# A decoder layer's head: x loaded first and turned at once, ada loads of 256 columns, five of eight rows summed on VectorE

## Chip, core, metric

One core of one Trainium2 chip runs the whole kernel. The metric is the device time of one execution in microseconds (us), the median of the runs shown. The engines are TensorE (PE; its weight loads PEld), VectorE (DVE), ScalarE (ACT), GpSimd (POOL) and SyncE (SP), which issues nearly all loads.

## What is computed

One decoder layer on x of 256 tokens by 1024 features in float32. The change is in the first lines: six vectors of 1024 come from the conditioning vector c, two of them (shift and scale) modulate the normed x, and the result u goes into one combined projection.

```
c_act = jax.nn.silu(c)
mod = (c_act @ w_ada[l] + b_ada[l])[:, None, :]
sh1, sc1, g1, sh2, sc2, g2 = jnp.split(mod, 6, axis=-1)
u = modulate(rmsnorm(h, norm1[l]), sh1, sc1)      # x * (1.0 + scale) + shift
h = h + g1 * token_mixer(u, w_in[l], ...)         # proj = u @ w_in, then retention, latent attention, merge
u = modulate(rmsnorm(h, norm2[l]), sh2, sc2)
h = h + g2 * hier_moe(u, ...)                     # top group, top-2 experts, SwiGLU
return rmsnorm(h, final_norm)
```

## The kernel before

The kernel is one long program for five in-order queues. The features are cut into eight chunks k of 128. The **head** is the loop `for k in range(8)` with what stands ahead of it: for each k it needs u of chunk k (256 tokens), made from x's chunk turned by TensorE (`x_turned`), from shift and scale of that chunk (`ada_mm`, `mod_of`), and from `u_of`, in which ScalarE scales (L444) and rounds to a high part (L446) and VectorE subtracts to a low part (L447). The weights of w_in are split in the same way (`split`: ScalarE L458 the high part, VectorE L459 the low part). Each product is three matmuls, high by high, low by high, high by low. In round k there are twelve matmuls of 352 columns (`mm3`, L373 to L375, in two halves n = 0 and 1) and twelve of 256 columns (`feat_mm`, L525 to L527).

Shift and scale of a chunk are a product of c_act with a 1024 x 256 piece of w_ada: one 1 MB buffer that holds 128 columns of shift and 128 of scale for all eight rows j (128 numbers of c each). TensorE does it as eight matmuls (L419) in four column groups that run side by side, the column of c_act being one of 32 columns, the rest zero; VectorE copies the result (L422), TensorE turns it (L435), VectorE reduces it over the four groups (L437) and applies norm and bias (L438, L440).

Loads stand in a list in program order and are issued by SP as buffers come free (27 buffers of 1 MB). At the start: ada of chunk 0, then x, then for each k ada of chunk k + 1 and the two pieces of w_in (`e0`, `e1`). On TensorE nine matmuls on ones, and eight more behind the first ada matmuls (`keep_warm`, `WARM0`), do no useful work. The order on TensorE in the loop is written out by hand, that on VectorE and ScalarE ahead of the loop too; in the loop a scheduler orders VectorE and ScalarE. The rest of the layer (attention, retention, merge, experts) isn't edited.

Of the kernel before, what the change touches and what calls it, by code (L numbers as in the profile page):

```python
# [43 lines left out]

WARM0 = 9, 8
WARM2 = 2
WARM3 = 1
WARM4 = 0
# [12 lines left out]
def const_tables():  # L61
# [143 lines left out]
def body(ctx, tc, A, out, plan=None):  # L205
# [207 lines left out]

    def ada_mm(k, pa):

        ev = ev_s.t[:, 256 * (k % 2):256 * (k % 2 + 1)]
        t = LD.get(("ada", k)).t.rearrange("p (k n) -> p k n", k=8)
        for j in range(8):
            i = T.matmul(pa.t[32 * (j % 4):32 * (j % 4) + 32, :256], csb[:, j, :], t[:, j, :], start=j < 4, stop=j >= 4,  # L419
                         skip_group_check=True, tile_position=(0, 32 * (j % 4)))  # L420
        LD.done(("ada", k))
        V.tensor_copy(ev, pa.t[:, :256])  # L422
        return ev, i.ins

    def x_turned(k):
        px = bank()
        for b in range(2):
            T.transpose(px.t[:, b * 128:(b + 1) * 128], xh[:, b, k * 128:(k + 1) * 128], ident)
        return px

    last_u = [None]

    def mod_of(k, pa, ev):
# [3 lines left out]
        V.tensor_reduce(sc, pa.t[:, 256:512].rearrange("p (i j r) -> p i j r", i=2, j=4)[:, :, :, 0], AX.X, ALU.add)  # L437
        V.scalar_tensor_tensor(acl[:, k:k + 1], sc[:, 1:2], bsc1[:, k:k + 1], colt[:, 8 + k:9 + k], op0=ALU.add,  # L438
                               op1=ALU.mult)
        V.tensor_add(shc[:, k:k + 1], sc[:, 0:1], colt[:, 16 + k:17 + k])  # L440
        pa.free()

    def u_of(k, px):
        last_u[0] = S.activation(uf[:, k, :], px.t[:, 0:256], AF.Identity, bias=shc[:, k:k + 1], scale=acl[:, k:k + 1]).ins  # L444
# [3 lines left out]
        px.free()  # L448

# [57 lines left out]

    scaled(0, 0, 128)
    scaled(1, 0, 128)
    scaled(0, 128, 384)  # L510
    scaled(1, 128, 1024)
    u_of(0, x_turned(0))
# [18 lines left out]
    for k in range(8):  # L531
# [6 lines left out]

        if 0 < k < 7:
            px, pa = x_turned(k + 1), bank()  # L540
            ev = ada_mm(k + 1, pa)[0]
        for n in range(2):
            s, hi, lo = hl[n]
            for b in range(2):
                mm3(eacc[n][b].t[:, :352], u_blk(k, b), (hi[:, 0, :], lo[:, 0, :]), k == 0, k == 7)
            s.free()
            if (n, k) == (0, 0):
                start.close()
                early = ExitStack()
                early.enter_context(tc.manual_schedule(engines={T.engine}))  # L550
                px = x_turned(1)
# [1128 lines left out]
```

## Time and profile before

| | |
|---|---|
| median of 3 runs | 524.14 us (523.97 to 524.57) |
| profiled execution | 524.77 us, its span 523.0 us, mean granted clock 0.993 |
| TensorE busy | 496.2 us, 95% of the span |
| VectorE, ScalarE busy | 282.5 us (54%), 197.9 us (38%) |
| moved by DMA | 175.42 MB, 335 GB/s in the mean |

The profile is of one execution; times in it run from the start of its span. A busy TensorE isn't one at its peak, since matmuls are pipelined and overlap in the rows. [...]

### The profile page before, as it was taken

How to read it: one execution, taken by the hardware profiler on the slowest of the kernel's cores; microseconds unless marked ns; L12 is line 12 of the kernel's file. 1: busy time of each engine (PE TensorE's matmuls, PEld its weight loads, DVE VectorE, ACT ScalarE, POOL GpSimd, SP SyncE). 2: the span in 40 equal slices, each digit the busy share in tenths (PEclk: the TensorE clock that was granted, in tenths of full speed). 3: DMA queues.
4: the chain of work that ended last, by engine and by line, in shares of the span. 5: the costliest groups of instructions: out<-in, count | busy, mean ns of one | idle time of the engine just before them, and what ended most of it. 6: DMA issues, size and time to landing. Idle time of an engine off the chain costs nothing.

```text
span 523.0 us, 9335 instructions
## 1 busy us (share of the span) xinstructions
PE 496.2 (95%) x3819; PEld 357.8 (68%) x3819; DVE 282.5 (54%) x524; ACT 197.9 (38%) x365; POOL 57.2 (11%) x50
## 2 busy tenths in 40 slices
PE   6999999999999999999999999999999989898984
PEld 2778999997887899999999887443334343434332
DVE  2455789883796978968956846413031213122113
ACT  2545873445677544556434524202020211111013
POOL 1000311411000001119800000000000000000000
PEclk8999999999999999999999999999999999999998
DMA  9999899788867781998697998999999999998994
GB/s 272 322 319 362 290 362 398 280 330 313 312 236 248 264 312 74 370 356 310 236 387 268 358 346 308 416 397 422 419 419 419 419 418 419 419 420 328 388 350 130
DMA packets 69778, 175.42 MB, mean 335 GB/s; under 512 B 5437, under 2 KB 27106, under 8 KB 60006
## 3 DMA queue, kind: packets, MB, share of 16 engines
q1 hardware_dynamic: 67136, 174.01, 89.7%
q10 hardware_dynamic: 2598, 0.79, 0.6%
q8 instruction: 31, 0.51, 0.4%
q14 instruction: 13, 0.11, 0.1%
HBM read 173.74 MB, written 1.05 MB: 334 GB/s over the span
## 4 chain that ended last, share of the span: by engine, by line
PE 80%; DVE 7%; DMA 4%; ACT 2%; SPq 2%; issue 2%; POOL 1%; ACTq 0%; DVEq 0%; POOLq 0%
PE b L1379 11%; PE b L527 6%; PE b L525 6%; PE b L526 6%; PE b L1482 6%; PE b L373 5%; PE b L375 5%; PE b L1320 5%; PE b L374 5%; PE b L1491 5%; DVE s L459 2%; DMA s<-in_w 2%; DMA s<-in_w_in 2%; PE b L1331 1%; PE b L1513 1%
## 5 line engine op out<-in xcount | busy, mean ns | idle before, releaser
L459 DVE TENSOR_TENSOR s<-s,s 128x1024 fp32r<-128x1024 f32 (+2 forms) x92 | 107.9, 1185 | 44.6 <-ACT s L458 44.4
L458 ACT ACTIVATE s<-s 128x1024 fp32r<-128x1024 f32 (+2 forms) x92 | 83.4, 921 | 85.1 <-PE b L527 50.4
L525 PE MATMUL b<-s,s 128*128 128x256 f32 x384 | 110.1, 287 | 0.0
L527 PE MATMUL b<-s,s 128*128 128x256 f32 x384 | 109.1, 284 | 0.7 <-DVE s L459 0.7
L526 PE MATMUL b<-s,s 128*128 128x256 f32 x384 | 108.7, 283 | 0.0
L527 PEld LDWEIGHTS b<-s,s 128*128 128x128 f32 x384 | 73.5, 192 | 1.4 <-DVE s L459 1.4
L526 PEld LDWEIGHTS b<-s,s 128*128 128x128 f32 x384 | 73.7, 192 | 0.4 <-issue 0.2
L525 PEld LDWEIGHTS b<-s,s 128*128 128x128 f32 x384 | 73.6, 192 | 0.4 <-issue 0.2
L1379 PE MATMUL b<-s,s 128*32 128x256 f32 x1024 | 61.8, 381 | 1.0 <-DMA s<-in_w 1.0
L1379 PEld LDWEIGHTS b<-s,s 128*32 128x32 f32 x1024 | 32.2, 110 | 32.9 <-issue 10.4
L373 PE MATMUL b<-s,s 128*128 128x512 f32 (+2 forms) x130 | 50.9, 392 | 1.1 <-ACT s L458 1.0
L375 PE MATMUL b<-s,s 128*128 128x512 f32 (+2 forms) x130 | 48.8, 375 | 0.0
L374 PE MATMUL b<-s,s 128*128 128x512 f32 (+2 forms) x130 | 48.3, 372 | 0.0
L1043 DVE SCALAR_TENSOR_TENSOR s<-s,cs,s 128x1024 f32<-128x1024 f32 x32 | 41.4, 1293 | 0.3
L1463 ACT ACTIVATE wr<-b 128x256 f32<-128x256 f32 x8 | 3.1, 383 | 87.0 <-PE b L1379 82.2
L1482 PE MATMUL b<-s,wr 128*32 128x512 f32 x224 | 32.8, 596 | 0.0
L1320 PE MATMUL b<-s,sml 128*128 128x512 f32 x56 | 27.2, 605 | 5.3 <-DVE sml L1316 5.3
L373 PEld LDWEIGHTS b<-s,s 128*128 128x128 f32 x130 | 24.5, 188 | 10.7 <-ACT s L458 4.4
L1314 DVE TENSOR_TENSOR S<-cst,rk 128x128 f32<-128x128 f32 x16 | 4.1, 287 | 48.9 <-PE b L1433 48.9
L1464 DVE SCALAR_TENSOR_TENSOR wr<-wr,b 128x256 f32<-128x256 f32 x8 | 3.3, 416 | 45.4 <-ACT wr L1463 45.4
L1111 POOL TENSOR_TENSOR s<-s,s 128x1024 f32<-128x1024 f32 x8 | 26.2, 3308 | 13.5 <-DMA s<-in_w_out 13.5
L375 PEld LDWEIGHTS b<-s,s 128*128 128x128 f32 x130 | 24.4, 188 | 4.5 <-DVE s L459 0.5
(254 smaller groups left out, 663.0 us busy)
## 6 DMA issues: line engine op xcount, KB each, us to landing
s<-in_w SPq DMA_DIRECT2D x92, 1024.0 KB
s<-in_w_in SPq DMA_DIRECT2D x22, 1024.0 KB
s<-in_w_ada SPq DMA_DIRECT2D x16, 1024.0 KB
s<-in_w_ada SPq DMA_DIRECT2D x16, 512.0 KB
s<-in_w_mla_o SPq DMA_DIRECT2D x4, 1024.0 KB
s<-in_w_ret_o SPq DMA_DIRECT2D x4, 1024.0 KB
s<-in_w_out SPq DMA_DIRECT2D x4, 1024.0 KB
s<-in_w SPq DMA_DIRECT2D x6, 512.0 KB
```

Source lines behind the costliest of these rows:

```text
L373: T.matmul(o, l[0], r[0], start=start, stop=False, skip_group_check=True)
L374: T.matmul(o, l[1], r[0], start=False, stop=False, skip_group_check=True)
L375: return T.matmul(o, l[0], r[1], start=False, stop=stop, skip_group_check=True)
L458: S.activation(hi, src, AF.Copy)
L459: V.tensor_tensor(lo, src, hi, ALU.subtract)
L525: T.matmul(o, hi[:, f], mh, start=k == 0 and c == 0, stop=False, skip_group_check=True)
L526: T.matmul(o, hi[:, f], ml, start=False, stop=False, skip_group_check=True)
L527: T.matmul(o, lo[:, f], mh, start=False, stop=k == 7, skip_group_check=True)
L1043: V.scalar_tensor_tensor(a, t[:, kk, :], cs[:, k:k + 1], a, op0=ALU.mult, op1=ALU.add)
L1320: T.matmul(pg[k4].t, Sr[:, b], hp[:, b, 4 * k4:4 * k4 + 4, :].rearrange("p k q -> p (k q)"), start=b == 0, stop=b == 1, skip_group_check=True)
L1379: i = T.matmul(ph.t[32 * j:32 * j + 32, m * 256:(m + 1) * 256], ug[:, k, 32 * j:32 * j + 32], w, start=k == 0, stop=k == 7, skip_group_che ...
L1482: T.matmul(py[n].t[32 * j:32 * j + 32, :], hdT[:, k, 32 * j:32 * j + 32], ts[j][:, k, n * 512:(n + 1) * 512], start=k == 0, stop=k == 1, s ...
```

## The change

x is loaded ahead of everything else on SP. The matmuls on ones behind the first ada matmuls go (`WARM0 = 9, 0`). x is scaled in three pieces, and all eight chunks are turned ahead of the loop, two per bank, and copied into the u buffer (chunk 0 stays in its bank). Chunks 0 and 1 of shift and scale come as before; of the other six, a pair of chunks comes in one load of 256 columns, for shift (s = 0) or scale (s = 1): key `(s, i)` for the chunks 2i and 2i + 1, `EARLY[k]` the keys that round k works on. For five of these six loads VectorE multiplies five of the eight rows j by their c_act and adds them up in place (`ada_v`), and TensorE does three rows and, with a column of ones, the sum (`ada_mm` with d = 5: four matmuls instead of eight); (0, 1) alone is done by eight. ScalarE copies the result. u of the two chunks of a pair can be made once both their loads are through. VectorE's order in the loop is now written out by hand.

```
-WARM0 = 9, 8
+WARM0 = 9, 0
+EARLY = (), ((0, 1), (1, 1)), ((0, 2),), ((1, 2),), ((0, 3),), ((1, 3),), (), ()
+EARLY_V = {(0, 1): 0}
+EARLY_D = 5
...
+    def ld_ada_pair(s, i):
+
+        def fn(t):
+            v = t.rearrange("p (h k n) -> p h k n", h=2, k=4)
+            c = s * 1024 + i * 256
+            for h in range(2):
+                Q.dma_start(v[:, h], w_ada[:, 4 * h:4 * h + 4, c:c + 256])
...
-    LD.add(("ada", 0), ld_ada_early(0))
-    LD.issue()
     for b in range(2):
         Q.dma_start(x[:, b, :], A["x"][0, b * 128:(b + 1) * 128, :])
+    LD.add(("ada", 0), ld_ada_first(0))
+    LD.issue()
...
     for k in range(8):
-        if k < 7:
-            LD.add(("ada", k + 1), ld_ada_early(k + 1))
+        if EARLY[k][:-1]:
+            LD.add(("ada", *EARLY[k][0]), ld_ada_pair(*EARLY[k][0]))
         LD.add(("e0", k), ld_k(w_in[:, k:k + 1, 4096:4800]))
         LD.add(("e1", k), ld_k(w_in[:, k:k + 1, 0:512]))
+        if k == 0:
+            LD.add(("ada", 1), ld_ada_first(1))
+        for a in EARLY[k][-1:] if k < 2 else EARLY[k]:
+            LD.add(("ada", *a), ld_ada_pair(*a))
...
+    def ada_v(key, d):
+
+        t = LD.get(key).t.rearrange("p (k n) -> p k n", k=8)
+        for j in range(8 - d, 8):
+            if j == 8 - d:
+                V.tensor_scalar(t[:, j, :], t[:, j, :], cs[:, j:j + 1], None, op0=ALU.mult)
+            else:
+                V.scalar_tensor_tensor(t[:, 8 - d, :], t[:, j, :], cs[:, j:j + 1], t[:, 8 - d, :], op0=ALU.mult, op1=ALU.add)
+
+    def ada_mm(key, pa, d=0):
...
+        m = 9 - d if d else 8
+        for j in range(m):
+            l = ones[:, 0:32] if j == 8 - d else csb[:, j, :]
+            T.matmul(pa.t[32 * (j % 4):32 * (j % 4) + 32, :256], l, t[:, j, :], start=j < 4, stop=j >= m - 4,
+                     skip_group_check=True, tile_position=(0, 32 * (j % 4)))
+        LD.done(key)
+        (S.copy if d else V.tensor_copy)(ev, pa.t[:, :256])
+        return ev
...
+    cuts = 0, 256, 512, 1024
+    for c0, c1 in zip(cuts, cuts[1:]):
+        scaled(0, c0, c1)
+        scaled(1, c0, c1)
+    px0 = turned(0)
+    pa0 = bank()
+    ev0 = ada_mm(("ada", 0), pa0)
+    V.tensor_copy(uf[:, 1, :], px0.t[:, 256:512])
+    turned(1, S)
+    mod_of(0, pa0, ev0)
+    u_of(0, px0.t[:, 0:256])
...
-        if 0 < k < 7:
-            px, pa = x_turned(k + 1), bank()
-            ev = ada_mm(k + 1, pa)[0]
+        if k == 0:
+            sums = []
+        elif k % 2 == 0 and k < 7:
+            u_of(k + 1)
+        for key in EARLY[k]:
+            ada_v(("ada",) + key, EARLY_V.get(key, EARLY_D))
+
+        def early_sums():
+            for key in EARLY[k]:
+                d = EARLY_V.get(key, EARLY_D)
+                pb = bank()
+                sums.append((*key, pb, ada_mm(("ada",) + key, pb, d)))
+
+        def mods():
+            while sums:
+                mod_pair(*sums.pop())
+            if k % 2 and k < 7:
+                u_of(k + 1)
+
         for n in range(2):
...
-            if n == (k == 0) and k < 7:
-                mod_of(k + 1, pa, ev)
-                u_of(k + 1, px)
+            if k > 1:
+                (mods if n else early_sums)()
...
+        if k == 1:
+            early_sums()
+            mods()
```

Three places in the queues. The first is TensorE from the row vectors' transpose to the first projection matmul. Before (L481 the row vectors, L419 ada, L382 on ones, L435 the sums' transposes, L428 x's; of the eight pairs of L382 one stands here, and k = 1's first x and ada follow k = 0's transposes):

```order
L481 MATMUL b_164<-cst,s_65 128x37
L419 MATMUL b_169<-s_69,s_65 32x256 x8
L382 LDWEIGHTS oneb
L382 MATMUL b_179<-oneb 128x512
...
L435 MATMUL b_169<-cst,s_65 128x128 x2
L428 MATMUL b_204<-cst,s_148 128x128 x2
L428 MATMUL b_244<-cst,s_148 128x128 x2
L419 MATMUL b_213<-s_101,s_65 32x256 x8
L373 MATMUL b_228<-s_210,s_149 128x352
```

Of the change (L530 the row vectors, L464 x's transposes, L454 ada, L471 the sums' transposes, L394 the first projection matmul):

```order
L530 MATMUL b_162<-cst,s_65 128x37
L464 MATMUL b_180<-cst,s_146 128x128 x4
L454 MATMUL b_185<-s_71,s_65 32x256 x8
L464 MATMUL b_196<-cst,s_146 128x128 x4
L471 MATMUL b_185<-cst,s_65 128x128 x2
L464 MATMUL b_213<-cst,s_146 128x128 x4
L464 MATMUL b_219<-cst,s_146 128x128 x4
L394 MATMUL b_228<-s_210,s_147 128x352
```

The first ada matmuls have moved behind x's first four transposes, and twelve more transposes stand ahead of the first projection matmul.

The second place is VectorE in a round. Before, k = 3 (L459 the low parts of w_in, L422 the copy of the ada sums, L437 to L440 shift and scale, L447 the low part of u):

```order
L459 TENSOR_TENSOR s_333<-s_118,s_333 128x352
L459 TENSOR_TENSOR s_336<-s_118,s_336 128x352
L422 COPY s_65<-b_347 128x256
L459 TENSOR_TENSOR s_339<-s_120,s_339 128x512
L437 TENSOR_REDUCE sml<-b_347 128x2
L438 SCALAR_TENSOR_TENSOR acl<-sml,bsc_167,colt 128x1
L440 TENSOR_TENSOR shc<-sml,colt 128x1
L447 TENSOR_TENSOR s_149<-s_100,s_149 128x256
```

Of the change, k = 2 and the beginning of k = 3 (L497 the low part of u, L508 those of w_in, L442 and L444 `ada_v`, L473 and L481 shift):

```order
L497 TENSOR_TENSOR s_147<-s_100,s_147 128x256
L508 TENSOR_TENSOR s_356<-s_118,s_356 128x352
L508 TENSOR_TENSOR s_359<-s_118,s_359 128x352
L508 TENSOR_TENSOR s_362<-s_120,s_362 128x512
L497 TENSOR_TENSOR s_147<-s_100,s_147 128x256
L442 TENSOR_SCALAR s_122<-s_122,cs 128x256
L444 SCALAR_TENSOR_TENSOR s_122<-s_122,cs 128x256 x4
L473 TENSOR_REDUCE sml<-b_383 128x2
L481 TENSOR_TENSOR shc<-sml,colt 128x2
L508 TENSOR_TENSOR s_413<-s_125,s_413 128x352
L508 TENSOR_TENSOR s_416<-s_125,s_416 128x352
L508 TENSOR_TENSOR s_419<-s_127,s_419 128x512
```

The copy has gone to ScalarE, and the multiply and four multiply-adds of a round's pair stand behind the low parts of the same round's weights and, in an even round, behind two low parts of u.

The third place is between the rounds k = 1 and k = 2, and ScalarE behind it. TensorE of the change, from the last matmul of k = 1 to the ones matmul in k = 2 (`one` is the column of ones; L394 to L396 are `mm3`):

```order
L454 MATMUL b_328<-s_108,s_65 32x256 x8
L454 MATMUL b_338<-s_115,s_65 32x256 x3
L454 MATMUL b_338<-s_115,one 32x256
L471 MATMUL b_338<-cst,s_65 128x128 x2
L471 MATMUL b_328<-cst,s_65 128x128 x2
L394 MATMUL b_228<-s_356,s_147 128x352
...
L454 MATMUL b_383<-s_122,s_65 32x256 x3
L454 MATMUL b_383<-s_122,one 32x256
L394 MATMUL b_230<-s_359,s_147 128x352
```

ScalarE of the change at the same place (L457 the copies of the sums, L493 u, L496 its high part, L507 the high parts of w_in):

```order
L457 COPY s_65<-b_338 128x256
L493 ACTIVATE s_100<-s_100,shc,acl 128x256 x2
L496 ACTIVATE s_147<-s_100 128x256 x2
L507 ACTIVATE s_416<-s_125 128x352
L507 ACTIVATE s_413<-s_125 128x352
L457 COPY s_65<-b_383 128x256
L507 ACTIVATE s_419<-s_127 128x512
```

Behind the ada matmuls of k = 1 TensorE has nothing but four transposes ahead of k = 2; in k = 2 the ones matmul, which reads VectorE's sum, stands between the two halves of `mm3`; and on ScalarE two u stand ahead of the first high part, and the copy of the sums of k = 2 ahead of the last high part of k = 3.

## Rows read from the trace of the kernel before

**Rows 1.** Windows: length, busy time of PE, PEld, DVE, ACT, POOL; PEclk, DMA share, GB/s.

```profile
36.96:42.14 5.18, 5.18 (x48) 4.17 (x45) 2.79 (x9) 2.53 (x6) 0.00 (x0) 1.00 1.14 321
14.92:54.60 39.68, 38.63 (x314) 32.02 (x315) 21.84 (x63) 20.55 (x41) 0.95 (x1) 1.00 1.12 338
```

**Rows 2.** Timeline of the start: start, us, engine, line, operation, [idle before and releaser].

```profile
7.53 1.94 PE L419 MATMUL b<-s,s 128*32 128x256 f32 x16
...
7.86 0.17 DVE L485 TENSOR_SCALAR bsc<-colt 128x8 f32<-128x8 f32 x1
...
11.28 0.16 DVE L497 TENSOR_REDUCE sml<-sml 128x2 f32<-128x4 f32 x1
...
12.53 0.80 ACT L506 ACTIVATE s<-s,sml 128x128 f32<-128x128 f32 x2 [2.10 <-POOL sml L363]
...
14.38 1.01 ACT L458 ACTIVATE s<-s 128x352 fp32r<-128x352 f32 x2
...
14.92 0.43 PE L373 MATMUL b<-s,s 128*128 128x352 f32 x1
```

**Rows 3.** Windows around the rise of TensorE's clock, columns as in rows 1.

```profile
10.00:10.50 0.50, 0.50 (x3) 0.15 (x1) 0.50 (x3) 0.44 (x2) 0.00 (x0) 0.52 1.22 291
10.50:11.00 0.50, 0.50 (x3) 0.20 (x2) 0.50 (x3) 0.00 (x0) 0.00 (x0) 1.00 1.20 288
```

**Rows 4.** Timeline where k = 2 begins (26.38), and of round k = 4.

```profile
26.38 0.43 PE L373 MATMUL b<-s,s 128*128 128x352 f32 x1 [1.05 <-ACT s L458]
...
36.79 0.96 DVE L459 TENSOR_TENSOR s<-s,s 128x352 fp32r<-128x352 f32 x2 [1.28 <-ACT s L458]
36.96 0.43 PE L373 MATMUL b<-s,s 128*128 128x352 f32 x1
...
38.00 0.68 DVE L459 TENSOR_TENSOR s<-s,s 128x512 fp32r<-128x512 f32 x1
...
38.62 0.17 DVE L437 TENSOR_REDUCE sml<-b 128x2 f32<-128x8 f32 x1
...
38.96 0.15 DVE L440 TENSOR_TENSOR shc<-sml,colt 128x1 f32<-128x1 f32 x1
...
39.21 0.56 ACT L444 ACTIVATE s<-b,shc,acl 128x256 f32<-128x256 f32 x1 [1.48 <-DVE shc L440]
...
39.39 0.28 PE L525 MATMUL b<-s,s 128*128 128x256 f32 x1
...
39.80 0.42 ACT L446 ACTIVATE s<-s 128x256 fp32r<-128x256 f32 x1
...
40.25 0.42 DVE L447 TENSOR_TENSOR s<-s,s 128x256 fp32r<-128x256 f32 x1 [1.14 <-ACT s L446]
...
40.83 0.38 PE L428 MATMUL b<-cst,s 128*128 128x128 f32 x2
41.14 1.07 PE L419 MATMUL b<-s,s 128*32 128x256 f32 x16
...
42.14 0.43 PE L373 MATMUL b<-s,s 128*128 128x352 f32 x1
```

**Rows 5.** Single lines: duration in ns, least, median and most; span of starts; forms.

```profile
L1043 DVE SCALAR_TENSOR_TENSOR s<-s,cs,s x32: 1253/1278/1757, 83.8 to 225.4; 128x1024 f32<-128x1024 f32 x32
...
L504 DVE TENSOR_SCALAR s<-s,sml x2: 285/482/679, 12.5 to 12.7; 128x128 f32<-128x128 f32 x1, 128x896 f32<-128x896 f32 x1
...
L506 ACT ACTIVATE s<-s,sml x3: 402/492/814, 12.5 to 15.3; 128x128 f32<-128x128 f32 x1, 128x256 f32<-128x256 f32 x1, 128x640 f32<-128x640 f32 x1
```

**Rows 6.** Windows with loads of 512-byte runs, then 1 KB runs; columns vary.

```profile
9.00:12.00 3.00, 3.00 (x18) 1.11 (x10) 1.97 (x7) 0.83 (x4) 0.20 (x1) 0.75 1.21 298
...
503.00:504.00 1.00, 1.00 (x9) 1.00 1.09 348
```

**Rows 7.** The load queue's waits, 90 to 330 us: total us, times, longest.

```profile
SPq L249 <- DVE s L459: 101.0, 22, 10.7
```

**Rows 8.** TensorE's waits, 55 to 320 us, the costliest line.

```profile
PE b L527 <- DVE s L459: 0.7, 3, 0.4
```

More of the change, by code (lines that the diff above doesn't have):

```diff
@@ L236, in body, with ld_ada_first @@
     S.dma_start(cst, A["cst"])
-    def ld_ada_early(k):
+    def ld_ada_first(k):
         def fn(t):
@@ L241, in fn @@
                 Q.dma_start(v[:, :, s, :], w_ada[:, :, s * 1024 + k * 128:s * 1024 + (k + 1) * 128])
+        return fn
+    def ld_ada_pair(s, i):
[4 more added lines that the diff above has]
+                Q.dma_start(v[:, h], w_ada[:, 4 * h:4 * h + 4, c:c + 256])
         return fn
@@ L412, in body, with x_turned, sums_of @@
     acl = st.tile([128, 8], F32, name="acl")
[L414 to L426, printed above, removed]
+    ev_n = [0]
+    def ada_v(key, d):
[6 more added lines that the diff above has]
+    def ada_mm(key, pa, d=0):
+        ev_n[0] += 1
+        ev = ev_s.t[:, 256 * (ev_n[0] % 2):256 * (ev_n[0] % 2 + 1)]
+        t = LD.get(key).t.rearrange("p (k n) -> p k n", k=8)
+        m = 9 - d if d else 8
[6 more added lines that the diff above has]
+        return ev
+    def x_turned(k, px=None):
+        px = px or bank()
         for b in range(2):
-            T.transpose(px.t[:, b * 128:(b + 1) * 128], xh[:, b, k * 128:(k + 1) * 128], ident)
+            T.transpose(px.t[:, (k % 2 * 2 + b) * 128:(k % 2 * 2 + b + 1) * 128], xh[:, b, k * 128:(k + 1) * 128], ident)
         return px
     last_u = [None]
-    def mod_of(k, pa, ev):
+    def sums_of(pa, ev):
         for i in range(2):
@@ L437, in mod_of, with mod_pair @@
         V.tensor_reduce(sc, pa.t[:, 256:512].rearrange("p (i j r) -> p i j r", i=2, j=4)[:, :, :, 0], AX.X, ALU.add)
+        pa.free()
+        return sc
+    def mod_pair(s, i, pa, ev):
+        k2 = slice(2 * i, 2 * i + 2)
+        sc = sums_of(pa, ev)
+        if s == 0:
+            V.tensor_add(shc[:, k2], sc, colt[:, 16 + 2 * i:18 + 2 * i])
+        else:
+            V.tensor_add(sc, sc, bsc1[:, k2])
+            V.tensor_mul(acl[:, k2], sc, colt[:, 8 + 2 * i:10 + 2 * i])
+    def mod_of(k, pa, ev):
+        sc = sums_of(pa, ev)
         V.scalar_tensor_tensor(acl[:, k:k + 1], sc[:, 1:2], bsc1[:, k:k + 1], colt[:, 8 + k:9 + k], op0=ALU.add,
@@ L440, in mod_of, with u_of @@
         V.tensor_add(shc[:, k:k + 1], sc[:, 0:1], colt[:, 16 + k:17 + k])
-        pa.free()
-    def u_of(k, px):
-        last_u[0] = S.activation(uf[:, k, :], px.t[:, 0:256], AF.Identity, bias=shc[:, k:k + 1], scale=acl[:, k:k + 1]).ins
+    def u_of(k, src=None):
+        last_u[0] = S.activation(uf[:, k, :], uf[:, k, :] if src is None else src, AF.Identity, bias=shc[:, k:k + 1],
+                                 scale=acl[:, k:k + 1]).ins
         hi, lo = hi_lo("u", k)
@@ L506, in scaled, with turned @@
             S.activation(xh[:, 0, c0:c1], x[:, 0, c0:c1], AF.Copy, scale=rst[:, 0:1])
[L508 to L512, printed above, removed]
+    def turned(i, eng=None):
+        px = x_turned(2 * i + 1, x_turned(2 * i))
+        if eng is None:
+            return px
+        copy(eng, uf[:, 2 * i:2 * i + 2, :], px.t.rearrange("p (k t) -> p k t", k=2))
+        px.free()
+    cuts = 0, 256, 512, 1024
[9 more added lines that the diff above has]
+    u_of(0, px0.t[:, 0:256])
+    px0.free()
     hl0 = [split(early_w(0)[0], 352)]
-    pa = bank()
-    ev = ada_mm(1, pa)[0]
-    keep_warm(WARM4)
+    turned(2, V)
+    turned(3, S)
     hl0.append(split(early_w(0)[1], 352))
-    scaled(0, 384, 1024)
     def feat_mm(accs, hi, lo, mh, ml, k):
@@ L547, in body @@
             if (n, k) == (0, 0):
+                pa = bank()
+                ev = ada_mm(("ada", 1), pa)
                 start.close()
                 early = ExitStack()
-                early.enter_context(tc.manual_schedule(engines={T.engine}))
-                px = x_turned(1)
-            if n == (k == 0) and k < 7:
-                mod_of(k + 1, pa, ev)
-                u_of(k + 1, px)
+                early.enter_context(tc.manual_schedule(engines={T.engine, V.engine}))
+            if (n, k) == (1, 0):
+                mod_of(1, pa, ev)
+                u_of(1)
+            if k > 1:
+                (mods if n else early_sums)()
         if k == 0:
```

5 lines of the change are left out of this document (removed).

## The prediction

> **What bounds the kernel now.** I read first the windows, then the waits, then the timeline of the stretch that the change edits. From the first projection matmul at 14.92 us to the last of k = 7 at 54.60 us TensorE is busy for 38.63 of 39.68 us, at full clock [rows 1]; its one wait there, 1.05 us, ends at 26.38 [rows 4]. So the head is TensorE-bound, although the DMA share beside it is 1.12 [rows 1]. One steady round k takes from 36.96 to 42.14, 5.18 us [rows 4]: twelve matmuls of 352 columns, the two transposes of the sums among them, up to 39.39; twelve of 256 columns up to 40.83 (1.44 us, 0.12 each); two x transposes (0.31 us) up to 41.14; the eight ada matmuls (1.0 us) up to 42.14. VectorE is busy for only 2.79 of these 5.18 us [rows 1], and its chain has slack: the sums are reduced at 38.62, u is scaled from 39.21 and rounded from 39.80, the low part is done at 40.67, and TensorE asks for it at 42.14 [rows 4].
>
> What comes behind hides nothing of a late head. Between 55 and 320 us TensorE's costliest wait is 0.7 us in total, for VectorE [rows 8], and the load queue spends 101 us between 90 and 330 us waiting for VectorE to release buffers [rows 7]: the transfers follow the computation, so the head's end moves the end of the program by almost the same amount.
>
> **Loads.** Columns in runs of 128 (512 bytes) came at 298 GB/s, runs of 256 columns (the last weights, 1 KB) at 348 GB/s [rows 6]. Six of eight megabytes of ada change from the one to the other: 1.048 MB in 3.0 us instead of 3.5, 3 us less transfer in all. The one wait of 1.05 us is all that the old head gave to late data, so it is the most that this can give by itself. By the new order, counted at these rates from 2.7 us on, the pair (1,1) is there at about 22.7 us, (0,2) at 27.4, the last chunk at 44.6: each before the walk below asks for it, so loads price at nothing; if they ran at 298 GB/s it would still be so.
>
> **The start.** x now comes first, but the row vectors still precede its squares on VectorE; they are done at 8.03 [rows 2], if they land as before. With two squares of 0.6 the sum is reduced at 9.15 (before 11.28) and x scaled from 10.4 (before 12.53, as far behind the reduction) [rows 2]. That is 2.1 us gained. What follows is longer. Before, the first ada matmuls ran at 7.53, in the wait for x [rows 2]; now they stand behind x's first four transposes in TensorE's queue (first pair of orders). With the eight warming matmuls gone, TensorE is idle until then. [...] So: a scaled piece of 256 columns 0.49 [rows 5], to 10.9; four transposes at the low clock 0.9, to 11.9; ada 1.94 as in the row at 7.53, to 13.9; four more transposes to 14.8 (the copy of the sums, 0.42, is under them); the two of the sums to 15.1; from the end of these to u 0.7 (reduce 38.62 to u 39.21 is 0.59, and 0.1 ahead [rows 4]); u 0.56 and its high part 0.42 to 16.8; the weights' high part 0.50 (two took 1.01 [rows 2]): first projection matmul at **17.3, 2.4 us later than 14.92**.
>
> **k = 0 and 1.** k = 0 needs 5.3 us (ada 1.0, 3.4 for its projections, 0.3 for two transposes, 0.5 of waits for u and its low part): first matmul of k = 1 at 22.6. k = 1 has no ada matmuls between its projections; both its pairs come behind the last of them. Two times 12 matmuls with 0.5 us of waits for low parts 2.6, then 1.44, ada of (0,1) 1.0, the four of (1,1) 0.55: to 28.2. Then TensorE has only four small transposes until u of k = 2 is there (third place of the orders): ScalarE's copy 0.5 with its hop, transposes to 29.0, on VectorE reduce, add, multiply, reduce, add (0.17 and 0.15 each [rows 4], 0.04 between) to 29.85, on ScalarE two u and then the high parts (0.5, 0.4, 0.4; the second u stands ahead of the first high part) to 31.15. k = 2 begins at 31.2. Of the 3.0 us of this seam 0.44 are work. Before, k = 0 and 1 took from 14.92 to 26.38 [rows 2, 4], 11.5 us with the wait of 1.05; now 13.9: **2.4 us more**.
>
> **Rounds 2 to 5.** Each TensorE round sheds 0.5 us (four of eight ada matmuls) and 0.31 us (x transposes). VectorE gains, for one pair, one multiply and four multiply-adds of 128x256. The multiply: 128 columns took 0.285 and 896 took 0.679 [rows 5], so 0.35. The multiply-add of this width isn't in the trace. The same operation of 1024 columns takes 1.278 [rows 5]; plain subtracts of 512 and 256 columns take 0.68 and 0.42 [rows 4], about 1.04 ns a column, so 768 columns less are 0.80 less, which gives **0.48**. Bounds: 0.32 (a quarter of 1.278) and 0.68 (the 512-column subtract [rows 4]). Each waits for the one before it, 0.035 apart: 0.35 + 4 x 0.515 = 2.4 us for a pair.
>
> [...]
>
> Summed alone, VectorE would fit (2.79 + 2.4 = 5.2 us a round). But its queue is in order, and TensorE asks for the sum after the first six matmuls of the same round. In an even round the second pair of orders shows what VectorE does between the high part of u and the last multiply-add: low part of u 0.43, three low parts of weights 0.53, 0.53, 0.68, the low part of the other u 0.43, each 0.09 overlapped (two of 0.53 took 0.96 [rows 4]), then the 2.4: 4.6 us. TensorE in that time has six matmuls and three ada matmuls, 2.0 us with the waits for low parts. It waits **2.6 us**, at 31.2 + 2.0; then 2.9 us for the rest: k = 3 at 38.7. In an odd round the high part of its third weight piece stands on ScalarE behind the copy of the even round's sums (36.5), so VectorE has the three low parts at 39.1 and the sum at 41.5: TensorE waits **1.3 us**, and once more **0.5 us** at its end, since the sums are turned only behind twelve matmuls and two u and a high part (1.3 us) follow reduce, add and multiply: k = 4 at 44.9. **A pair of rounds takes 13.7 us.** Before, two rounds took 10.36 (twice 5.18): **6.7 us more** for rounds 2 to 5. k = 6 and 7 have no ada and take 7.6; before they had what is left of 26.38 to 54.60 behind four rounds, 7.5.
>
> **The sum.** 2.4 + 2.4 + 6.7 + 0.1 = 11.6 us: k = 7 ends at 66.2 instead of 54.6. VectorE has little to do in the last 7 us of the head and may start the next stage earlier; of the waits for it there [rows 8] I give back 0.6. So 11.0 us. The profiled execution took 524.77 us (span 523.0), the median is 524.14: I expect a profile of 535.8 and a median of **535.1 us**. The 0.48 carries 1.6 us for each 0.1 (16 multiply-adds that TensorE waits for): 0.32 gives 532.5, 0.68 gives 538.3. The start is good to 1 us either way.
>
> **Rivals.** *TensorE stays the bound (faster).* Five pairs shed 0.5 us each, seven x transposes of 0.31 leave the rounds: 2.5 + 2.2 less, the later start 2.4 more, 2.3 us in favour: 521.8. For it speaks that VectorE's busy time fits a round. It decides by one thing: a pair of rounds must take less than 10.3 us, so the sum must be there when six matmuls are done, and the order puts five low parts ahead of it. 8 in 100. *The sums cost almost nothing, the seams stay.* If VectorE ran multiply-adds at once, the seam behind k = 1, the start and 0.5 us at each odd end remain: 5 us, 529. 13 in 100. *The clock rises later.* [...] 6 in 100. [...] *The delay is given back behind the head*, because loads run ahead meanwhile: within 0.2%, which is 1.05 us and about what a measurement of this kernel can tell from no change. Against it stand the queue's waits for buffers [rows 7]. 5 in 100.
>
> **How the numbers follow.** The walk as it stands has 68 in 100, with a range of its own from 531.5 to 539 (0.32 to 0.68 and the start's 1 us). With the 13 and the 6, slower has 87, the same 5, faster 8. The range 528.5 to 539.5 holds the walk, the seams alone and half of the later clock, some 82 in 100.
>
> **What the profile would show.** Right: the first projection matmul near 17.3; TensorE idle for 2.5 us ahead of k = 2, for VectorE's multiply-add in each of k = 2 to 5 (2.6, 1.3, 2.6, 1.3), all of k = 7 done near 66; the rounds behind it as before. Wrong, if the waits for the multiply-adds are missing (then the price 0.48 or the order of VectorE is misread), or if TensorE's waits behind 70 us or the load queue's waits shrink by as much as the head lost.

## The result, and the profile after

The changed kernel is slower, as forecast, but by more than twice as much: 549.94 us in the median of four runs (545.6 to 552.7) against 524.31 of the kernel before, a ratio of 1.048 with a 95% interval of 1.0452 to 1.0509. The forecast was 535.1, its range up to 539.5. The profiled execution, the slowest of the four, took 552.7 us (span 551.0, mean granted clock 0.979). Its span is 28.0 us longer than that of before, and it splits so (the same points of the program in both traces; round k is the pass of the head's loop for chunk k, and round 6 begins 7.5 us ahead of the head's end):

| stretch | before | after | more | forecast |
|---|---|---|---|---|
| to the first projection matmul | 14.92 | 17.77 | 2.9 | 2.4 |
| rounds 0 and 1 | 11.46 | 14.52 | 3.1 | 2.4 |
| rounds 2 to 5 | 20.85 | 32.93 | 12.1 | 6.7 |
| from round 6 (47.23, now 65.22) to the third matmul of the values' up-projection (103.9, now 124.3) | 56.7 | 59.1 | 2.4 | -0.5 |
| on to the last expert's first products (502.06, now 522.76) | 398.2 | 398.5 | 0.3 | 0 |
| on to the last products of w2 (506.90, now 533.09) | 4.8 | 10.3 | 5.5 | 0 |
| on to the span's end | 16.1 | 17.9 | 1.8 | 0 |

The timeline of TensorE in the changed kernel, the rows that answer to [rows 2, 4]; in brackets the idle time ahead of a row and who ended it:

```profile
11.30 1.12 PE L464 MATMUL b<-cst,s 128*128 128x128 f32 x4 [3.57 <-ACT s L551]
12.35 1.94 PE L454 MATMUL b<-s,s 128*32 128x256 f32 x16
14.21 1.12 PE L464 MATMUL b<-cst,s 128*128 128x128 f32 x4
...
17.77 0.43 PE L394 MATMUL b<-s,s 128*128 128x352 f32 x1 [0.88 <-ACT s L507]
...
32.29 0.42 PE L394 MATMUL b<-s,s 128*128 128x352 f32 x1 [2.20 <-ACT s L496]
...
36.91 1.06 PE L454 MATMUL b<-s,one 128*32 128x256 f32 x2 [1.18 <-DVE s L444]
...
44.66 0.62 PE L454 MATMUL b<-s,one 128*32 128x256 f32 x2 [1.38 <-DVE s L444]
...
48.81 0.43 PE L394 MATMUL b<-s,s 128*128 128x352 f32 x1 [0.73 <-ACT s L496]
...
53.42 0.82 PE L454 MATMUL b<-s,one 128*32 128x256 f32 x2 [2.25 <-DVE s L444]
...
61.07 0.62 PE L454 MATMUL b<-s,one 128*32 128x256 f32 x2 [1.16 <-DVE s L444]
...
65.22 0.42 PE L394 MATMUL b<-s,s 128*128 128x352 f32 x1 [0.72 <-ACT s L496]
```

Each wait of the forecast is there and at its place: for u behind round 1 (2.20), for VectorE's sum inside rounds 2 to 5 (5.97 together), at the odd rounds' ends (0.73, 0.72). Round 2's wait is 1.18 instead of the forecast 2.6 mostly because TensorE ran at the low clock up to it (a share of 0.50 from 33.5 us on): from the round's start to the sum it is 4.62 us, as foretold (2.0 + 2.6), and in round 4, at full clock, 4.61 with a wait of 2.25. The price of a multiply-add was right too, 485 ns where 0.48 us had been worked out (ns, least, median, most):

```profile
L444 DVE SCALAR_TENSOR_TENSOR s<-s,cs x20: 483/485/487, 25.5 to 60.5; 128x256 f32<-128x256 f32 x20
```

What the forecast didn't have stands in the windows (columns as in [rows 1]; PEclk, the granted share of TensorE's clock, is the third column from the end). In two stretches of the head, each behind a wait of over 2 us, the granted clock is 0.50; ahead of the first TensorE had run nothing but four transposes in 3.4 us (28.9 to 32.3). The two waits of 1.38 and 1.16 us have none behind them.

```profile
34.00:40.00 6.00, 4.82 (x18) 2.68 (x17) 2.71 (x7) 1.78 (x4) 0.00 (x0) 0.50 1.08 361
...
54.00:57.00 3.00, 3.00 (x12) 2.76 (x12) 0.17 (x1) 0.90 (x2) 0.00 (x0) 0.50 0.66 187
```

Behind the head TensorE waits twice for the scaled latent, and at the end once for what the view calls the last weights:

```profile
82.46 0.33 PE L844 MATMUL b<-cst,s 128*128 128x128 f32 x1 [1.04 <-ACT s L827]
83.91 1.74 PE L844 MATMUL b<-cst,s 128*128 128x128 f32 x9 [1.12 <-ACT s L827]
...
533.09 3.64 PE L1670 MATMUL b<-s,wr 128*32 128x256 f32 x32 [6.34 <-DMA s<-in_w]
```

### The profile page after: what moved, and what is told of

Same layout as the page of the kernel before. It is cut to its first block, busy times and chain, and to the rows that moved or that the text cites. A ratio compares the mean times of both kernels' runs of the same rounds, so it can differ in the third digit from the quotient of the medians.

```text
span 551.0 us, 9258 instructions
## 1 busy us (share of the span) xinstructions
PE 505.6 (92%) x3767; PEld 363.4 (66%) x3771; DVE 293.4 (53%) x544; ACT 200.1 (36%) x372; POOL 59.4 (11%) x50
## 4 chain that ended last, share of the span: by engine, by line
PE 79%; DVE 7%; DMA 5%; ACT 3%; issue 3%; POOL 1%; SPq 0%; ACTq 0%; DVEq 0%; POOLq 0%
PE b L1458 10%; PE b L584 6%; PE b L582 6%; PE b L583 6%; PE b L1561 6%; PE b L394 5%; PE b L396 5%; PE b L395 5%; PE b L1399 5%; PE b L1570 4%; DMA s<-in_w 4%; DVE s L508 2%; DVE s L444 1%; PE b L1410 1%; PE b L454 1%
## 5 line engine op out<-in xcount | busy, mean ns | idle before, releaser
L508 DVE TENSOR_TENSOR s<-s,s 128x1024 fp32r<-128x1024 f32 (+2 forms) x92 | 108.0, 1193 | 36.5 <-ACT s L507 36.4
L507 ACT ACTIVATE s<-s 128x1024 fp32r<-128x1024 f32 (+2 forms) x92 | 83.9, 923 | 100.9 <-PE b L584 57.3
L584 PEld LDWEIGHTS b<-s,s 128*128 128x128 f32 x384 | 74.1, 193 | 0.8 <-DVE s L508 0.8
L582 PEld LDWEIGHTS b<-s,s 128*128 128x128 f32 x384 | 74.4, 194 | 0.4 <-issue 0.2
L583 PEld LDWEIGHTS b<-s,s 128*128 128x128 f32 x384 | 74.2, 193 | 0.4 <-issue 0.2
L394 PE MATMUL b<-s,s 128*128 128x512 f32 (+2 forms) x130 | 51.6, 397 | 4.8 <-ACT s L496 3.9
L396 PE MATMUL b<-s,s 128*128 128x512 f32 (+2 forms) x130 | 49.9, 384 | 0.0
L395 PE MATMUL b<-s,s 128*128 128x512 f32 (+2 forms) x130 | 49.4, 380 | 0.1
L394 PEld LDWEIGHTS b<-s,s 128*128 128x128 f32 x130 | 25.1, 193 | 14.8 <-ACT s L496 4.7
L396 PEld LDWEIGHTS b<-s,s 128*128 128x128 f32 x130 | 25.2, 194 | 5.1 <-DVE s L508 1.3
L395 PEld LDWEIGHTS b<-s,s 128*128 128x128 f32 x130 | 25.2, 194 | 4.3 <-DVE s L497 1.1
```

Source lines behind the costliest of these rows:

```text
L394: T.matmul(o, l[0], r[0], start=start, stop=False, skip_group_check=True)
L395: T.matmul(o, l[1], r[0], start=False, stop=False, skip_group_check=True)
L396: return T.matmul(o, l[0], r[1], start=False, stop=stop, skip_group_check=True)
L507: S.activation(hi, src, AF.Copy)
L508: V.tensor_tensor(lo, src, hi, ALU.subtract)
L582: T.matmul(o, hi[:, f], mh, start=k == 0 and c == 0, stop=False, skip_group_check=True)
```

## The experiments

Twelve kernels, each timed in five rounds beside the kernel before, whose medians lay between 524.27 and 524.64. "Jump" is the time of TensorE's sequencer in the branch that steps over the block for overflowing experts, explained below; the other columns are starts in us on the timeline of each profile.

| kernel | first projection | round 2 | round 6 | jump | median (runs) |
|---|---|---|---|---|---|
| before | 14.92 | 26.38 | 47.23 | 0.35 | 524.3 |
| changed | 17.77 | 32.29 | 65.22 | 6.66 | 549.94 (545.6 to 552.7) |
| e1 no sums | 17.03 | 31.95 | 56.52 | 0.35 | 535.92 (535.6 to 536.7) |
| e2 sums ahead | 17.20 | 31.72 | 56.55 | 5.69 | 543.25 (538.3 to 544.9) |
| e3 clock held | 18.24 | 32.77 | 63.79 | 0.35 | 542.55 (541.7 to 543.8) |
| e4 one root first | 18.36 | 32.88 | 65.05 | 6.62 | 551.00 (545.4 to 552.4) |
| e5 code shift | 15.54 | 30.30 | 61.42 | 0.69 | 542.97 (541.3 to 543.4) |
| e6 ada first | 16.06 | 30.81 | 63.67 | 0.61 | 544.05 (543.2 to 544.9) |
| e7 seam inside | 17.16 | 30.07 | 62.83 | 0.67 | 542.50 (541.3 to 543.9) |
| e8 three repairs | 17.18 | 30.33 | 52.69 | 0.46 | 534.27 (532.9 to 534.6) |
| e9 roots first | 16.28 | 31.04 | 61.98 | 0.68 | 544.21 (541.8 to 545.2) |
| e10 all repairs | 16.92 | 30.08 | 51.73 | 0.45 | 532.89 (530.9 to 533.2) |
| e11 before, x first | 17.50 | 27.82 | 47.80 | 0.35 | 524.75 (524.1 to 525.4) |
| e12 pad behind | 16.99 | 31.51 | 62.61 | 6.62 | 549.71 (548.9 to 552.2) |

**e1, no sums on VectorE.**

```
-EARLY_D = 5
+EARLY_D = 0
```

> No partial sums on VectorE: every pair of chunks is turned by eight matmuls, with the copies on VectorE; loads and the early x as in the changed kernel, nothing left out. Queue theory: the four waits of TensorE for the multiply-add (6.0 us together) and the low clock (0.50) that follows two of them go; the copy between rounds 1 and 2 still has its wait of about 2 us. The head then ends at 60 to 63 instead of 72.7, and the run takes 536 to 541. Load theory (the pairs land late and the waits for the multiply-add are only where this shows): TensorE waits as long, now for the loads, the head ends at 69 or later, and the run takes 546 to 550. The stage behind the head keeps its extra 2.3 us by either.

Measured: 535.92 us, ratio 1.0221 (1.0207 to 1.0234). TensorE's only waits of over 0.6 us from the start of round 2 to that of round 6 are these three rows of its timeline:

```profile
31.95 0.66 PE L394 MATMUL b<-s,s 128*128 128x352 f32 x1 [2.13 <-ACT s L496]
45.49 0.43 PE L394 MATMUL b<-s,s 128*128 128x352 f32 x1 [0.65 <-ACT s L496]
56.52 0.42 PE L394 MATMUL b<-s,s 128*128 128x352 f32 x1 [0.65 <-ACT s L496]
```

No wait for loads took the place of the four for the sums, so the loads aren't late, and the queue theory stands. Rounds 2 to 5 take 24.57 instead of 32.93: the sums cost 8.4 us, their own waits of 6.0 and what came with these. The median fell by 14.0; the rest is mostly the jump, which no theory had then, so that the median came within 0.1 us of the foretold range (536 to 541) is in part chance. One thing foretold didn't happen: the clock still reads 0.50 from 32 to 37.5 us, and the first row above takes 0.66 us instead of 0.43, so the wait for u ahead of round 2 was enough here for the first low stretch, without any wait for a sum.

**e2, the same sums a round earlier in VectorE's queue.**

```
-        for key in EARLY[k]:
+        for key in (EARLY[k] if k < 3 else ()) + (EARLY[k + 1] if 1 < k < 7 else ()):
             ada_v(("ada",) + key, EARLY_V.get(key, EARLY_D))
```

> From round 3 on each sum stands one round ahead in VectorE's queue; VectorE does the same work, and nothing is left out. Queue theory (it is the place of the sum, not its size): the waits of rounds 3, 4 and 5 (1.38, 2.25 and 1.16 us) go, with them the low clock at 53.4 to 57; round 2 keeps its wait. The head ends 6 to 7 us earlier, at about 66, and the run takes 542 to 544. Size theory (VectorE has too much work in a round): TensorE waits as long for the splits of the weights instead, the head ends within 2 us of 72.7, and the run takes 548 to 551.

Measured: 543.25 us, 1.0339 (1.0298 to 1.038). The timeline of TensorE keeps the wait of round 2 and loses those of rounds 3, 4 and 5:

```profile
36.34 1.06 PE L454 MATMUL b<-s,one 128*32 128x256 f32 x2 [1.17 <-DVE s L444]
46.22 0.43 PE L394 MATMUL b<-s,s 128*128 128x352 f32 x1 [0.72 <-ACT s L496]
56.55 0.43 PE L394 MATMUL b<-s,s 128*128 128x352 f32 x1 [0.73 <-ACT s L496]
```

VectorE does all that it did, and the sums cost nothing from round 3 on: their place in the queue was the price, not their size. Rounds 4 and 5 take 10.33 us, each pair's end with a wait of 0.7 in the rows above; in e1, without sums, they take 11.03 (45.49 to 56.52), and before they took 10.27 (36.96 to 47.23). The head gains more than foretold, 8.7 us at round 6 instead of 6 to 7.

**e3, the waits filled with matmuls on ones.**

```
+FILLW = {(0, 2): 12, (1, 2): 6, (0, 3): 12, (1, 3): 6}
...
         for j in range(m):
+            if d and j == 8 - d and key != ("ada", 1, 1):
+                keep_warm(FILLW[key[1:]])
...
         if k == 1:
             early_sums()
             mods()
+            keep_warm(10)
```

> Ten matmuls on ones are put behind the scale of round 1, and twelve or six ahead of the last of each pair's matmuls in rounds 2 to 5, where TensorE waits; they only fill the waits, and nothing is left out. Clock theory: the waits stay as long, but the granted clock stays at 1.00 from 33 to 41 and from 53 to 58, and the head ends 4 to 6.5 us earlier, at 66 to 69; the run takes 543.5 to 546. Rival (the low stretches don't come from the waits, or the filled matmuls take what the clock gives back): the head ends at 71.5 or later and the run takes 548.5 to 551.

Measured: 542.55 us, 1.034 (1.0327 to 1.0354). The windows that read 0.50 in the changed kernel read 1.00:

```profile
34.00:40.00 6.00, 6.00 (x36) 3.32 (x35) 3.29 (x9) 1.79 (x4) 0.00 (x0) 1.00 1.08 362
...
54.00:57.00 3.00, 3.00 (x23) 2.98 (x24) 1.56 (x5) 1.14 (x3) 0.00 (x0) 1.00 0.98 339
```

So with the waits filled the clock stayed at 1.00. But it is worth less than expected: rounds 2 to 5 take 31.02 us instead of 32.93, and in the two even rounds the fills ran 0.41 us past the sum (5.02 us from the round's start to the sum instead of 4.61), 0.8 together, which gives the clock 2.7 us. The foretold 4 to 6.5 is missed: the head ends 1.4 us earlier, at 71.3, close to the rival's 71.5. The median is below its range all the same, because here too the jump is short.

**e4, one root ahead of the rope.** GpSimd's queue had changed without an edit there: the scheduler put the two reciprocal roots, which scale the latent, behind four rope operations instead of ahead of them.

```
+    live["mla"] = step(mla_it)
     rope_q0 = rope_post("q", 0)
...
-            for _ in range(SIDE[i]):
+            for _ in range(SIDE[i] - (i == 2)):
```

> The reciprocal root of the latent's norm stands ahead of the rope operations in GpSimd's queue, as before the change (one of its two operations behind one of rope's four); nothing is left out. If the four rope operations ahead of it are what the stage behind the head lost, that stage (20.8 us after the change, 18.5 before) is 2 to 2.5 us shorter, the low clock at 84.3 to 87.6 goes, and the run takes 546.5 to 548. If TensorE waits there for something else, or the rope is then late for its own reader, the stage stays at 20 to 21 us and the run at 549 to 551.

Measured: 551.0 us, 1.0469 (1.043 to 1.0508); no gain, as its second theory had it. The waits at L844 are gone from TensorE's timeline, but the scheduler moved VectorE's order with the root, and the splits of the up-projection weights (L869) are late instead:

```profile
86.77 0.38 PE L898 MATMUL b<-s,s 128*128 128x256 f32 x1 [0.87 <-DVE s L869]
...
101.77 0.39 PE L898 MATMUL b<-s,s 128*128 128x256 f32 x1 [1.93 <-DVE s L869]
```

**e5, TensorE's code moved by eight matmuls on ones.** The sequencers' rows of the line of the branch gave the wait at the end another reading: the four other engines leave it in 0.05 to 0.07 us, TensorE in 6.66.

```
-WARM0 = 9, 0
+WARM0 = 9, 8
...
     V.tensor_scalar(bsc1, colt[:, 24:32], 1.0, None, op0=ALU.add)
+    keep_warm(WARM0[1])
```

> Eight matmuls on ones more, in TensorE's wait for x at 7.7 to 11.3; they do nothing but hold the clock and move all of TensorE's later code by their own length; nothing is left out. In the changed kernel TensorE's sequencer spent 6.66 us in the jump over the block for overflowing experts (0.35 before the change and without the sums, where the code lies elsewhere). Code theory: the length of that jump hangs on where the code lies; it is back to about 0.35, the wait of 6.3 us ahead of the last products goes, all runs lie within 2 us of each other and the median is 545 to 546.5. Stream theory (the last weights are late, and the jump is only where it shows): the wait stays, and the runs lie between 545 and 552 as before. If the jump stays long, a shift of this length doesn't move the code across whatever matters, and the place of the code stays open.

**e12, the same eight behind the jump.**

```
     last_sum(4)
+    keep_warm(8)
```

> The control of the code shift: the same eight matmuls on ones, but behind the jump, among and after TensorE's last products, so that all code ahead of the jump and the jump's own target lie where they lay in the changed kernel; nothing is left out, and the end takes at most 0.5 us more. Code theory: the jump stays long in most runs, 5 to 7 us in the profile if that run has it, and the runs spread from 545 to 553. If eight matmuls more anywhere were enough (a longer program, another chip, another day), the jump is under 1 us and all runs lie within 2 us of 546.

Measured: e5 542.97 us, 1.0356 (1.0341 to 1.037), runs within 2.1 us of each other; e12 549.71, 1.0491 (1.0468 to 1.0514). The branch on TensorE's sequencer (ns, thrice the same since it runs once), first the changed kernel, then before, e5 and e12:

```profile
L1598 PEldq COMPARE_BRANCH  x1: 6658/6658/6658, 526.0 to 526.0; - x1
```

```profile
L1519 PEldq COMPARE_BRANCH  x1: 352/352/352, 505.3 to 505.3; - x1
```

```profile
L1599 PEldq COMPARE_BRANCH  x1: 685/685/685, 521.8 to 521.8; - x1
```

```profile
L1598 PEldq COMPARE_BRANCH  x1: 6622/6622/6622, 523.2 to 523.2; - x1
```

The same eight matmuls make the jump short ahead of it and leave it long behind it, so it is the place of the code and neither its length nor the late weights. The table fits without exception: all kernels that keep TensorE's program ahead of the jump as in the changed kernel (e2, e4, e12) have 5.7 to 6.7 us, all others at most 0.69. The traces have transfers of instructions on queue q8, 16 KB each. In the four kernels with the long jump none starts in the 15 us ahead of the jump and one falls inside it, 3.2 to 4.1 us after its start (at 530.1 us in the changed kernel); in the ten others the last one started 1.8 to 7.5 us ahead of it (at 497.8 us before). That the long jump waits for this transfer is the author's estimate, worked out from these times. The queue's row for the changed kernel's jump, 526.0 to 532.7 us (transfers, MB, share):

```profile
q8 instruction: 1, 0.02, 1.1%
```

The profile doesn't name the engine that such a transfer is for, and why the jump lasts 1.4 us beyond its landing isn't shown. With the code in this place the runs of a kernel spread over 3.3 to 7.1 us, in the other changed kernels over 1.1 to 3.4, which suggests that the jump's length varies from run to run; only one run of each was profiled.

In e5 the first projection came 2.2 us earlier as well, which wasn't expected: 0.4 because x was scaled earlier, the rest in TensorE's matmuls ahead of it. The rows of its start, against the first three of the changed kernel above:

```profile
10.89 0.66 PE L464 MATMUL b<-cst,s 128*128 128x128 f32 x4 [0.59 <-ACT s L552]
11.47 1.07 PE L454 MATMUL b<-s,s 128*32 128x256 f32 x16
12.47 0.66 PE L464 MATMUL b<-cst,s 128*128 128x128 f32 x4
```

The same 24 matmuls take 2.2 us from first to last instead of 4.0.

**e6, the first chunk ahead of x again.**

```
+    LD.add(("ada", 0), ld_ada_first(0))
+    LD.issue()
     for b in range(2):
         Q.dma_start(x[:, b, :], A["x"][0, b * 128:(b + 1) * 128, :])
-    LD.add(("ada", 0), ld_ada_first(0))
-    LD.issue()
```

(with its matmuls, eight on ones behind them, and its scale and shift ahead of x's squares, as before)

> The first chunk of shift and scale is loaded ahead of x again and its matmuls, with eight on ones behind them, stand ahead of x's transposes; the rest as in the changed kernel, nothing left out. If the order at the start is worth what the prediction gave it, the first projection starts at 15 to 16 instead of 17.8 and all that follows is 2 to 2.5 us earlier: 547 to 548 where the jump at the end stays long, 542.5 to 543.5 where it is short. If the pairs' loads bind instead, round 2 starts within 0.5 us of 32.3 as in the changed kernel and the run keeps its time.

Measured: 544.05 us, 1.0381 (1.0367 to 1.0395), first projection at 16.06, round 2 at 30.81: 1.7 and 1.5 us earlier than in the changed kernel, but no better than e5, which has x first; the median is 0.5 above the foretold 542.5 to 543.5 for a short jump. With eight matmuls on ones ahead of x's transposes no gain of the old order is left that these runs could show (15.54, 16.28 and 16.92 with x first, in e5, e9 and e10).

**e7, the first pair inside round 1.**

```
-EARLY_V = {(0, 1): 0}
+EARLY_V = {(0, 1): 0, (1, 1): 0}
...
-            if k > 1:
+            if k > 0:
                 (mods if n else early_sums)()
...
-        if k == 1:
-            early_sums()
-            mods()
```

> The first pair's shift and scale are turned inside round 1 (by eight matmuls each, no sum on VectorE) instead of behind it; nothing is left out. Place theory: round 2 starts at 28.5 to 30 instead of 32.3, the wait of 2.2 us there falls under 1 us, the clock doesn't fall behind it, and the head ends 4 to 6 us earlier, at 67 to 69. Load theory: the pair isn't there in time, TensorE waits inside round 1 for it, round 2 starts at 31 or later, and the head ends at 71 or later. The run is the changed kernel's less what the head gains, with the jump at the end long or short: 540 to 547.

Measured: 542.5 us, 1.0352 (1.0332 to 1.0371). Round 2 starts at 30.07, and the wait ahead of it is 0.70: the place theory, 0.07 beyond its late end. The gain isn't kept. VectorE's sum of round 2 still comes 4.61 us after the round's start (4.62 in the changed kernel), TensorE waits 2.24 instead of 1.18 there and its clock falls only there (1.00 from 15 to 33 us, 0.74 from 33 to 37), and round 6 comes 2.4 us earlier, with the start 0.6 of it, instead of 4 to 6.

**e8, three repairs: e6, e7 and the sums ahead, none in rounds 1 and 2.**

> Three edits at once: the first chunk ahead of x as before the change, the first pair turned inside round 1, and the sums of rounds 3 to 5 a round ahead in VectorE's queue, with no sum in rounds 1 and 2; nothing is left out. If the three waits add up, the head ends at 58 to 60 instead of 72.7, TensorE's clock stays at 1.00 through it, and the run takes 529 to 532 with a short jump at the end, 535 to 538 with a long one: still above before, by what the start, the seam and the stage behind the head keep. If VectorE's or ScalarE's queue makes a new wait of them, the head ends at 62 or later and the run takes 534 or more with a short jump.

Measured: 534.27 us, 1.0192 (1.0178 to 1.0206). Round 6 begins at 52.69, so the head ends at 60.2 (foretold 58 to 60), and the clock reads 1.00 in every window from 15 to 62 us. The run is 2 us above the range, in that of the rival: the start came at 17.18, 1.1 later than in e6 with the same order, and in round 2 TensorE has a new wait of 1.14 us for VectorE's copy of the sums.

**e9, both roots first, on top of e5.**

```
-    rope_q0 = rope_post("q", 0)
...
+    with tc.manual_schedule(engines={G.engine}):
+        live["mla"] = step(mla_it)
+        rope_q0 = rope_post("q", 0)
...
-            for _ in range(SIDE[i]):
+            for _ in range(SIDE[i] - (i == 2)):
```

> The kernel with eight more matmuls on ones at the start (542.97 us), and besides both reciprocal roots ahead of the rope operations in GpSimd's queue, as before the change; nothing is left out. Root theory: TensorE's two waits for the scaled latent (1.03 and 1.12 us) and the low clock behind them go, the stage from the head's last projection to the up-projections is 2 to 2.5 us shorter, and the run takes 540 to 541. Rival, after the run with one root ahead: VectorE's order moves along, its splits of the up-projection weights come late instead, TensorE waits for those, and the run takes 542 to 544.

Measured: 544.21 us, 1.0379 (1.0361 to 1.0398), e5's interval overlaps. The rival, 0.2 above its range: again 0.87 and 1.93 us at the splits of the up-projection.

**e10, all repairs together** (e5, e7, e9, the sums of e8, and ScalarE for the copy of round 2's shift).

> As the three repairs (534.27 us), but with x first and eight matmuls on ones at the start, ScalarE in place of VectorE for the copy that round 2 waited 1.14 us for, and both roots ahead of the rope; nothing is left out. First projection at 15.5 to 16.2 instead of 17.2, round 2 without a wait inside it, clock at 1.00 through the head. If the roots' order helps, 529 to 531; if it only moves the wait, 531 to 533. It stays above the kernel before (524.3) by either: the start keeps 0.6, round 1 eight matmuls more (1 us), and each pair of rounds a wait of 0.7 us for a chunk's split.

Measured: 532.89 us, 1.0159 (1.0145 to 1.0173), the upper of the two ranges. Its profile is 6.2 us longer than that of before: round 6 comes 4.5 us later, the stage behind takes 1.8 more.

**e11, the kernel before with x first.**

```
-    LD.add(("ada", 0), ld_ada_early(0))
-    LD.issue()
     for b in range(2):
         Q.dma_start(x[:, b, :], A["x"][0, b * 128:(b + 1) * 128, :])
+    LD.add(("ada", 0), ld_ada_early(0))
+    LD.issue()
```

> The kernel before the change with one edit: x is loaded ahead of the first chunk of shift and scale; the order of the work is as before, and nothing is left out. If the order of these two loads sets the start, the first chunk's matmuls come at 11 to 12.5 instead of 7.5, the first projection at 15.5 to 17 instead of 14.9, and the run takes 524.9 to 526.4. If the start is set by what stands between x and its first transposes and the loads only trade places, the first projection stays within 0.4 us of 14.9 and the run within 523.8 to 524.7.

Measured: 524.75 us, 1.0003 (0.9994 to 1.0012), no difference. Half of each theory: the first projection is later than foretold (15.5 to 17), at 17.50, and the run isn't. Its rounds 1 to 5 start at 22.83, 27.82, 32.81, 37.81 and 42.80, 4.99 apart, and round 6 at 47.80; those of before took 6.14, 5.32, 5.26, 5.18 and 5.09. The waits of ScalarE for the weights that it splits, first before, then e11 (total us, times, longest, 8 to 57 us):

```profile
ACT s L458 <- DMA s<-in_w_in: 7.8, 7, 2.5
```

```profile
ACT s L458 <- DMA s<-in_w_in: 2.6, 6, 0.7
```

Before, the rounds ran in step with the loads; a start that is 2.6 us later finds the data there, and gains all but 0.6 back by round 6. That the loads set the pace is read from these rows, not tried by itself.

## Why the prediction was wrong

**The start (2.4, measured 2.9)** was right in size, and so was its walk: from x's first transposes to the first projection it takes 6.47 us, where 6.4 were added up (10.9 to 17.3). It begins at 11.30 instead of 10.9; in the kernels with the same start (e1 to e4, e7, e12) it begins between 10.73 and 11.89. Some 1.8 of the 2.9 lie in slow matmuls: up to the second four transposes at 14.21 the rows take 1.12, 1.94 and 1.12 us, as in e10, whose clock reads 0.53 from 10 to 15 us. In e5, with eight matmuls on ones in the wait for x, they take 0.66, 1.07 and 0.66, the same stretch takes 4.65 and the first projection comes at 15.54, 0.6 behind before. But these eight don't make sure of it: in e9 and e10, which have them too, the first projection comes at 16.28 and 16.92, and e10's durations are as slow as without them. What sets e5 apart from e10 isn't shown. No run shows the 0.9 us of the walk for four transposes at a low clock: they took 1.12 here and 0.66 in e5. Nor does one show the later rise of the clock that the forecast gave 6 in 100: in round 0 the matmuls of 352 columns take 0.32 us, as in e5.

**Rounds 0 and 1 (2.4, measured 3.1)** were nearly right: the wait for u behind round 1 is the 2.2 us of the walk (29.0 to 31.2). Of the rest 0.2 lies in round 0 (5.51 for 5.3) and 0.4 between the last ada matmul and the end of the four transposes (1.17 for 0.8).

**Rounds 2 to 5 (6.7, measured 12.1)** is the largest error of the head, with two parts. The walk was short: a pair of rounds at full clock takes 15.1 us (e9's second pair, 46.87 to 61.98) where 13.7 were added up, so the two pairs cost 9.4 more than before. It lies in small steps: 3.26 us from an even round's sum to the next round (51.48 to 54.74 in e9) where 2.9 were taken, 3.07 (41.59 to 44.66) instead of 2.8 from an odd round's start to its sum, and 4.15 instead of 3.4 from there to the next round. And the step that had no term at all: **"TensorE waits 2.6 us"** was priced as 2.6 us, as if the engine went on as fast as before. The clock fell, 2.7 us more (32.93 less twice 15.1). The prediction had weighed the clock only for its first rise.

How much that costs isn't fixed by the program. In e12, the same program up to the jump, the clock reads 0.50 within these rounds only from 32 to 34.5 and from 52.5 to 55 us (matmuls of 352 columns take up to 0.66 and 0.50 us there, 0.32 outside), and rounds 2 to 5 take 31.10. The first of these stretches costs nothing there: its pair takes 15.10 (31.51 to 46.61), since TensorE only waits less for the sum behind it, 1.17. In e9 the clock falls behind one of three waits of this length (2.20, 2.25 and 2.25): it reads 0.61 from 37 to 41 us and 1.00 from 41 to 62.

**"I give back 0.6" (measured 2.4 more)** was wrong in sign. The stage behind the head got two waits of 1.1 us and a stretch at a granted clock of 0.50 (84.5 to 87.5 us). That stretch isn't the cause: e2 and e3 have the same two waits, their clock reads 1.00 all through the stage, and it takes as long (59.1). The scheduler had moved GpSimd's two roots, outside the diff: before they ran at 56.87 and 58.95 us, ahead of the rope's first operation at 60.29, now at 81.00, behind the four that begin at 75.08. The prediction gave that no price. But the roots alone aren't the cause: e4 and e9 put them back, and the wait went to VectorE's splits. The stage takes 58.5 to 60.4 us in all kernels with the change (56.7 before); which part of the scheduler's new order sets it stays open, and so does the cause of this error.

**Nothing at the end (measured 7.3)** is the largest single error, a term at nothing: the rule that a late head moves the end by the same amount holds up to the last expert (0.3 us in 398), and then the jump took 5.5 more, and the slow clock behind its wait (0.50 from 533.0 to 536.7 us, 1.00 before; 3.64 us for 32 matmuls, 1.94 before) 1.8. The trace of before has a short jump (0.35), and nothing in it says that this hangs on where the code lies. Without it the profiled execution of 552.7 us would have taken 545.4, still above the range.

**Loads at nothing, 0.48 for a multiply-add, VectorE's queue as the cause**: right, by e1 and e2. **"The head is TensorE-bound"** was half right: e11 shows 4.99 us a round when TensorE sets the pace, so the 5.1 to 5.3 of before held a little waiting for loads that the busy rows hide, and a later start alone is free there. In the changed kernel, whose loads come faster (359 to 365 GB/s from 15 to 30 us, 320 to 323 before), a start 2.2 us earlier brought round 2 2.0 us earlier (e5).

No version here beats the kernel before. The repairs win back 17 of the 25.6 us, and up to 7.3 of these 17 are the jump's, by where the code came to lie.

## What to carry to other kernels

Work for a half-idle engine is priced by its place in that engine's queue, not by its length: from round 3 to round 6 the head takes 23.6 us with the sums behind the round's own splits (1.3 of it a slow stretch), 15.6 with the same sums a round ahead (e2) and 16.6 without them (e1). A wait on the matmul engine can cost more than itself, since its clock may fall: here 2.7 us in one execution and 0.9 in another of the same program up to the jump, so a forecast with waits of 2 us needs such a term, as a range. A slow stretch ahead of a wait for another engine can cost nothing, as e12's first did (its pair of rounds took 15.10 us). Where a time moves that no edit explains, look at the sequencers' rows for the branches, and at a control that moves code and nothing else.

## What the runs showed of the hardware

One jump over unused code took TensorE's sequencer 0.35 to 0.69 us or 5.7 to 6.7 us by the place of the code alone, and the wait is then put down to a transfer (6.34 <- DMA) that had nothing to do with it. The granted clock reads 1.00 between 10 and 15 us in the changed kernel's windows although its matmuls there took as long (1.12, 1.94 and 1.12 us) as in e10 (1.11, 1.94, 1.12), where the same window reads 0.53. The changed kernel's trace has no clock record ahead of 16.2 us, and the view reads 1.00 where it has none: there the durations are the only sign.
